# Linear attention's memory laid out anew in a hybrid decoder step: gates, values, queries and keys over r's weights and buffers, W_o's pieces over the prompt attention's last buffers

## The chip, the core and the metric

The kernel runs on one core of one Trainium2 chip. The metric is the device time of the program in microseconds (us), the median of several runs; lower is better. TensorE (PE) does the matrix products, VectorE (DVE), ScalarE (ACT) and GpSimd (POOL) the elementwise work, SyncE (SP) issues most of the DMA transfers.

## What is computed

One layer of a decoder on a prompt of 2048 tokens (width 1024) and 8 sample tokens, all in float32. One projection of the normalised input is split among sliding-window softmax attention (`q_a`, `k_a`, `v_a`), gated linear attention (`q_g`, `k_g`, `v_g`, a swish gate `u_rg`, a low-rank forget gate `u_lr`). Their outputs are joined, go through `w_o` and a residual, and a SwiGLU network follows.

```python
u_qa, u_ka, u_va, u_qg, u_kg, u_vg, u_rg, u_lr = jnp.split(h @ w_in, idx, axis=-1)
...
log_a = jax.nn.log_sigmoid((u_lr @ w_gla_gate2 + b_gla_gate).astype(jnp.float32)) / GLA_TAU
...
def step(S, inp):                       # per chunk of tokens
    qc, kc, vc, ac = inp
    b = jnp.cumsum(ac, axis=2)
    o_inter = jnp.einsum('nhtd,nhdv->nhtv', qc * jnp.exp(b), S)
    diff = b[:, :, :, None, :] - b[:, :, None, :, :]
    decay = jnp.exp(jnp.where(causal[:, :, None], diff, -jnp.inf))
    scores = jnp.einsum('nhtd,nhsd,nhtsd->nhts', qc, kc, decay)
    o = o_inter + jnp.einsum('nhts,nhsv->nhtv', scores, vc)
...
g = rmsnorm(o_gla.astype(x.dtype), gla_norm_g).reshape(N, T, GLA_WIDTH) * jax.nn.silu(r_gla)
h = x + jnp.concatenate([o_attn.astype(x.dtype), g], axis=-1) @ w_o
z = rmsnorm(h, ffn_norm_g)
return h + (jax.nn.silu(z @ w_gate) * (z @ w_up)) @ w_down
```

## The kernel before

**Products.** A float32 operand is split into a rounded high part and the rest (`split`: a cast on ACT, L95, and a subtraction on DVE, L96). A dense product is three products into one bank of PSUM (`mm3`): high by high, high by low, low by high, L107, L108 and L109.

**Stages.** The first is prompt attention, 16 blocks of 128 tokens with the sample tokens: q, k and v of each block, the swish gate `r` (its weights lie in `WR`), scores (L358, L359), the exponential (L370), the division by the sum on POOL (L375, tile `S`), transposes of P (L386, bank `ps_p`) whose split halves go to `pT`, and the products with v (L390, L391, bank `po`). An output is scaled on DVE (`o`, L393) and stored (L394). The low-rank part `lr` of each pair of blocks, and `r`, go out to memory (`lr_d`, `r_d`). The second stage is linear attention, 8 pairs of 128 tokens, that is 256 tokens a pair. `front_b` makes what a pair needs: queries and keys (four output tiles of 24 products into `ps_qk`, copied to `qTb` at L700 and `kTb` at L702), the gates (`ps_g`, L719, from `lr`, a tile of three loads from `lr_d`; ACT's L721, L722 read the bank into `la` and `Bt`; L730 sums along the tokens) and the values (48 products into `ps_v` with `WV`, and for the first pair 16 more for the sample tokens, L747). `gla_b` goes through 7 levels (`E`, L797; a product with q on POOL, L811; four products into `ps_l`, L816; the result into `AT`), then makes the output (`po`, L865 from v and `AT`, L868 from the state) and updates the state. The next pair's front is interleaved by the planner. `split_wo` (L767 to L784) loads a piece of W_o into `wro`, splits it into `wohl` and stores it, a piece every half pair. Then come W_o's stage (its first mixed tile `mt` is cast by ACT's L95), the norm, and the network's three products.

**Memory.** SBUF is cut into pools on a left and a right stack. A pool that is closed gives its bytes back, and the next stage's tiles lie on them. The kernel opens its pools with `reuse_waits="tile"`: a tile over a closed pool's memory waits for the accesses of exactly the old tiles that lay at its bytes. Where a tile is laid therefore sets what it has to wait for.

**Order.** The order of each engine's queue isn't written by hand. A planner simulates the program (`schedule_with_timeline_sim=True`) and puts each engine's instructions into one queue by its own times; an engine then works off its queue in order, and an instruction that waits holds those behind it.

**Lines of the change.** L593 to L609 open the pools of linear attention; L652 to L669 make its constant tiles, among them `AT` (zeroed at L662), the two `lr` tiles `lr30` and `lr31` of 96 by 264 elements (L666, zeroed at L667) and `bd` (L671).

Of the kernel before, what the change touches and what calls it, by code (L numbers as in the profile page):

```python
# [11 lines left out]
F32R = mybir.dt.float32r  # L12
# [39 lines left out]
def hymba_kernel(ctx: ExitStack, tc: tile.TileContext, I, O, X=None, phases=3):  # L52
# [3 lines left out]
    def pool(stack, name, bufs, **kw):  # L56
        return stack.enter_context(tc.tile_pool(name=name, bufs=bufs, reuse_waits="tile", **kw))
# [534 lines left out]
    with ExitStack() as ph:  # L592
        pad = pool(ph, "b_pad", 1)  # L593
# [2 lines left out]
        wl = pool(ph, "b_wl", 2)  # L596
        dp = pool(ph, "b_dec", 1)
        lp = pool(ph, "b_lm", 1)
        gtp = pool(ph, "b_gt", 2)
        wk = pool(ph, "b_wk", 2)  # L600
        qkp = pool(ph, "b_qk", 2)
# [4 lines left out]

        wq1 = pool(ph, "b_wq1", 1, side="right")
        wq0 = pool(ph, "b_wq0", 1, side="right")
        wop = pool(ph, "b_wo", 1)  # L609
        aux = pool(ph, "b_aux", 2, space=PSUM)  # L610
        acc = pool(ph, "b_acc", 2, space=PSUM)
        lvp = pool(ph, "b_lv", 2, space=PSUM)
# [50 lines left out]
            ATs.append(AT)  # L663
        lr3s = []
        for i in range(2):
            lr3 = pad.tile([96, 264], F32R, name=f"lr3{i}")  # L666
            nc.gpsimd.memset(lr3.bitcast(F32), 0.0)  # L667
            lr3s.append(lr3)
        for i in range(3):  # L669
# [777 lines left out]
```

## Time and profile before

| | |
|---|---|
| median of 3 runs | 2285.05 us (2284.72 to 2285.94) |
| the profiled execution | 2284.49 us, its span 2282.5 us |
| PE, DVE, ACT, POOL busy | 97%, 69%, 44%, 27% of the span |
| end of attention's last product to the first gate product | 406.07 to 411.54 |
| first output product of linear attention | 448.75 |
| first product of W_o's stage | 727.14 |

Times inside the execution count from the start of the span, and a program's lines are those of the kernel above. A busy share alone doesn't say whether an engine is held: for that one reads the waits, a list of who waited for whom and how long, and the timeline, which has each instruction's start, its length, and in brackets the idle time just before it with what ended it. Instructions of a kind that follow each other stand in one row with a count.

### The profile page before, as it was taken

How to read it: one execution, taken by the hardware profiler on the slowest of the kernel's cores; microseconds unless marked ns; L12 is line 12 of the kernel's file. 1: busy time of each engine (PE TensorE's matmuls, PEld its weight loads, DVE VectorE, ACT ScalarE, POOL GpSimd, SP SyncE). 2: the span in 40 equal slices, each digit the busy share in tenths (PEclk: the TensorE clock that was granted, in tenths of full speed). 3: DMA queues.
4: the chain of work that ended last, by engine and by line, in shares of the span. 5: the costliest groups of instructions: out<-in, count | busy, mean ns of one | idle time of the engine just before them, and what ended most of it. 6: DMA issues, size and time to landing. Idle time of an engine off the chain costs nothing.

```text
span 2282.5 us, 34902 instructions
## 1 busy us (share of the span) xinstructions
PE 2206.6 (97%) x12697; PEld 1908.8 (84%) x12697; DVE 1567.7 (69%) x3076; ACT 1009.3 (44%) x2259; POOL 625.3 (27%) x706
## 2 busy tenths in 40 slices
PE   8999998899998999999999999999999899999997
PEld 6888887688897788688888889999999878787886
DVE  6787888567766466776666667676676675747486
ACT  5666777465565334332333333333333333434342
POOL 2443433455465133211111111011110122222222
PEclk9999999899999999999999999999999999999999
DMA  7323334245424889944242366233333377878777
GB/s 236 120 77 103 108 104 163 91 132 187 144 88 188 303 291 314 320 137 127 81 124 81 114 222 240 89 107 97 94 103 93 126 200 172 216 171 227 162 203 239
DMA packets 211992, 364.75 MB, mean 160 GB/s; under 512 B 15683, under 2 KB 129116, under 8 KB 208732
## 3 DMA queue, kind: packets, MB, share of 16 engines
q1 hardware_dynamic: 174764, 259.05, 34.7%
q0 software_dynamic: 37056, 103.47, 17.8%
q8 instruction: 100, 1.64, 0.3%
q14 instruction: 72, 0.59, 0.1%
HBM read 211.24 MB, written 152.29 MB: 159 GB/s over the span
## 4 chain that ended last, share of the span: by engine, by line
PE 82%; DMA 5%; DVE 5%; issue 3%; POOL 2%; ACT 2%; SPq 0%; POOLq 0%; DVEq 0%; ACTq 0%
PE ps_b L108 8%; PE ps_b L107 8%; PE ps_b L109 8%; PE ps_c L108 5%; PE ps_c L107 5%; PE ps_c L109 5%; PE ps_a L108 5%; PE ps_a L107 5%; PE ps_a L109 5%; PE ps_d L107 3%; PE ps_d L108 3%; PE ps_d L109 3%; PE ps_wo L107 3%; PE ps_wo L109 3%; PE ps_wo L108 2%
## 5 line engine op out<-in xcount | busy, mean ns | idle before, releaser
L109 PE MATMUL ps_b<-z,whl 128*128 128x258 f32 (+1 forms) x792 | 253.6, 320 | 2.1 <-DVE whl L96 2.1
L107 PE MATMUL ps_b<-z,whl 128*128 128x258 f32 (+1 forms) x792 | 254.3, 321 | 1.2 <-ACT whl L95 1.2
L108 PE MATMUL ps_b<-z,whl 128*128 128x258 f32 (+1 forms) x792 | 254.5, 321 | 0.0
L95 ACT CAST dm<-mr 128x384 fp32r<-128x384 f32 (+1 forms) x224 | 108.1, 488 | 190.6 <-PE ps_b L109 100.6
L108 PE MATMUL ps_a<-z,whl 128*128 128x258 f32 (+1 forms) x528 | 169.4, 321 | 0.0
L108 PE MATMUL ps_c<-z,whl 128*128 128x258 f32 (+1 forms) x528 | 169.4, 321 | 0.0
L109 PE MATMUL ps_a<-z,whl 128*128 128x258 f32 (+1 forms) x528 | 169.2, 320 | 0.0
L109 PE MATMUL ps_c<-z,whl 128*128 128x258 f32 (+1 forms) x528 | 169.1, 320 | 0.0
L107 PE MATMUL ps_c<-z,whl 128*128 128x258 f32 (+1 forms) x528 | 168.9, 320 | 0.2 <-DMA z<-zc_d_P 0.2
L107 PE MATMUL ps_a<-z,whl 128*128 128x258 f32 (+1 forms) x528 | 169.0, 320 | 0.0
L109 PEld LDWEIGHTS ps_b<-z,whl 128*128 128x128 f32 x792 | 149.6, 189 | 14.5 <-DVE whl L96 2.5
L107 PEld LDWEIGHTS ps_b<-z,whl 128*128 128x128 f32 x792 | 149.7, 189 | 13.0 <-ACT whl L95 1.3
L108 PEld LDWEIGHTS ps_b<-z,whl 128*128 128x128 f32 x792 | 149.6, 189 | 11.9
L96 DVE TENSOR_TENSOR dm<-mr,dm 128x384 fp32r<-128x384 f32 (+1 forms) x224 | 115.4, 519 | 61.4 <-ACT dm L95 61.4
L95 ACT CAST whl<-wrg 128x512 fp32r<-128x512 f32 x132 | 81.6, 620 | 155.7 <-PE ps_b L109 81.2
L983 DVE TENSOR_TENSOR gu<-ps_c,gu 128x512 f32<-128x512 f32 (+1 forms) x130 | 77.9, 600 | 56.7 <-PE ps_c L109 56.1
L96 DVE TENSOR_TENSOR whl<-wrg,whl 128x512 fp32r<-128x512 f32 x132 | 90.8, 689 | 36.6 <-ACT whl L95 36.2
L811 POOL TENSOR_TENSOR bd<-E,qTb 64x256 f32<-64x256 f32 x112 | 103.2, 922 | 44.3 <-DVE ebl L840 15.7
L1282 POOL DMA_DIRECT2D md_d<-m x22 | 15.6, 711 | 363.5 <-DVE m L1245 363.5
L95 ACT CAST whl<-sy 128x512 fp32r<-128x512 f32 x88 | 54.6, 620 | 132.2 <-PE ps_b L109 84.9
L107 PEld LDWEIGHTS ps_c<-z,whl 128*128 128x128 f32 x528 | 100.0, 189 | 8.5 <-issue 0.6
L107 PEld LDWEIGHTS ps_a<-z,whl 128*128 128x128 f32 x528 | 100.0, 189 | 7.9
(399 smaller groups left out, 6684.7 us busy)
## 6 DMA issues: line engine op xcount, KB each, us to landing
mr<-md_d SPq DMA_DIRECT2D x24, 1344.0 KB
zc_d_P<-zhl POOLq DMA_DIRECT2D x56, 512.0 KB, 6.4
z<-zc_d_P SPq DMA_DIRECT2D x14, 2048.0 KB
wrg<-in_w_gate_dram SPq DMA_DIRECT2D x44, 512.0 KB
wrg<-in_w_up_dram SPq DMA_DIRECT2D x44, 512.0 KB
nT_d<-nT SPq DMA_DIRECT2D x16, 1024.0 KB
zT<-nT_d SPq DMA_DIRECT2D x8, 2048.0 KB
h_d<-gu POOLq DMA_DIRECT2D x48, 256.0 KB, 4.7
```

Source lines behind the costliest of these rows:

```text
L95: nc.scalar.copy(h, src)
L96: (eng or nc.vector).tensor_tensor(l, src, h.bitcast(F32), ALU.subtract)
L107: nc.tensor.matmul(ps, lh, rh, start=start, stop=False, skip_group_check=more)
L108: nc.tensor.matmul(ps, lh, rl, start=False, stop=False, skip_group_check=more)
L109: nc.tensor.matmul(ps, ll, rh, start=False, stop=stop, skip_group_check=more)
L811: nc.gpsimd.tensor_tensor(bv[rows, h], E5[rows, :, :, 1], qv[rows, :, :, 1], ALU.mult)
L983: nc.vector.tensor_tensor(out, a, b, ALU.add)
L1282: nc.gpsimd.dma_start(md_d[sb][g][:, :, q, fp - GROUPS[g][0], :], src.rearrange("p (m t) -> p m t", m=4))
```

## The change

The pool `wop` of W_o's pieces (`wro`, `wohl`) is opened behind `lp` on the left stack, and no longer behind `wbv`, at the stack's top. Behind it a new pool, `lrp`, holds the two `lr` tiles, which lay in `pad` at the stack's bottom. Every other tile of linear attention on the left stack shifts. The computation is the same, and every instruction has its counterpart. Lines of the changed kernel stand 3 higher from L599 to L608, and 2 higher from L610 on.

```diff
@@ -596,6 +596,9 @@
         wl = pool(ph, "b_wl", 2)
         dp = pool(ph, "b_dec", 1)
         lp = pool(ph, "b_lm", 1)
+        wop = pool(ph, "b_wo", 1)
+
+        lrp = pool(ph, "b_lr", 1)
         gtp = pool(ph, "b_gt", 2)
         wk = pool(ph, "b_wk", 2)
         qkp = pool(ph, "b_qk", 2)
@@ -606,7 +609,6 @@
 
         wq1 = pool(ph, "b_wq1", 1, side="right")
         wq0 = pool(ph, "b_wq0", 1, side="right")
-        wop = pool(ph, "b_wo", 1)
         aux = pool(ph, "b_aux", 2, space=PSUM)
         acc = pool(ph, "b_acc", 2, space=PSUM)
         lvp = pool(ph, "b_lv", 2, space=PSUM)
@@ -663,7 +665,7 @@
             ATs.append(AT)
         lr3s = []
         for i in range(2):
-            lr3 = pad.tile([96, 264], F32R, name=f"lr3{i}")
+            lr3 = lrp.tile([96, 264], F32R, name=f"lr3{i}")
             nc.gpsimd.memset(lr3.bitcast(F32), 0.0)
             lr3s.append(lr3)
```

The bytes in each partition, and the tiles of prompt attention that lay there:

| tile | before | on | after | on |
|---|---|---|---|---|
| `lr30`, `lr31` | 28544 | bias | 91136 | 64 bytes of `rt`, `ks` |
| `scm` | 80960 | `qT` | 93248 | `ks`, `r` |
| `la` | 81984 | `qT`, `o` | 94272 | `r` |
| `Bt` | 84096 | `o`, `ol` | 96384 | `r`, `WR` |
| `v` | 88320 | `ol`, `rt`, `ks`, `r` | 100608 | `WR` |
| `qTb` | 96512 | `r`, `WR` | 108800 | `WR` |
| `kTb` | 100736 | `WR` | 113024 | `WR` |
| `WV` | 104960 | `WR`, `nT` | 117248 | `WR`, `nT` |
| `wro` | 137728 | `nT` | 78848 | `qT` |
| `wohl` | 141824 | `nT`, `qs`, `qn` | 82944 | `qT`, `o`, `ol`, `rt` |

`AT`, `bd`, `r`, `E` and their neighbours move 2112 bytes down. In W_o's stage, whose addresses stay, the first `mt` (113760 to 122016) lay on `WV` alone and now lies on `kTb` and `WV`.

The planner makes another order of this. On PE, around the first gate products (`ps_g`) and the first value products (`ps_v`), before:

```order
L386 MATMUL ps_p<-ident,S 128x128 x4
L391 MATMUL po<-pT,vp_194 128x512
L386 MATMUL ps_p<-ident,S 128x128 x4
L390 MATMUL po<-pT,vp_196 128x512
L391 MATMUL po<-pT,vp_196 128x512
L390 MATMUL po<-pT,vp_194 128x512
L391 MATMUL po<-pT,vp_194 128x512
L719 MATMUL ps_g<-lr_5008,w_130 128x264 x2
L107 MATMUL ps_v<-WV,zT 128x512
L108 MATMUL ps_v<-WV,zT 128x512
L109 MATMUL ps_v<-WV,zT 128x512
```

After:

```order
L386 MATMUL ps_p<-ident,S 128x128 x4
L721 MATMUL ps_g<-lr_5011,w_130 128x264 x2
L358 MATMUL ps_s<-kT_191,qT 128x256
L359 MATMUL ps_s<-kT_191,qT 128x256
L358 MATMUL ps_s<-kT_191,qT 128x256
L359 MATMUL ps_s<-kT_191,qT 128x256
L390 MATMUL po<-pT,vp_195 128x512
L391 MATMUL po<-pT,vp_195 128x512
L390 MATMUL po<-pT,vp_196 128x512
L107 MATMUL ps_v<-WV,zT 128x512
L108 MATMUL ps_v<-WV,zT 128x512
L109 MATMUL ps_v<-WV,zT 128x512
```

The gates and the values stood behind all of attention's products; now the gates stand ahead of its last four score products, and the values ahead of its last products with v.

On POOL, around the zeroing of the two `lr` tiles (`S`, `den` is attention's softmax, `r`, `rt` the swish gate), before:

```order
L375 TENSOR_TENSOR S<-S,den 128x1024 x2
L247 TENSOR_TENSOR r<-r,rt 128x512
L375 TENSOR_TENSOR S<-S,den 128x1024 x4
L658 MEMSET Sbd 128x512
L662 MEMSET AT_5004 128x1024
L662 MEMSET AT_5006 128x1024
L667 MEMSET lr_5008 96x264
L667 MEMSET lr_5010 96x264
```

After:

```order
L375 TENSOR_TENSOR S<-S,den 128x1024 x2
L247 TENSOR_TENSOR r<-r,rt 128x512
L375 TENSOR_TENSOR S<-S,den 128x1024 x2
L669 MEMSET lr_5011 96x264
L669 MEMSET lr_5013 96x264
L375 TENSOR_TENSOR S<-S,den 128x1024 x2
L660 MEMSET Sbd 128x512
L664 MEMSET AT_5007 128x1024
L664 MEMSET AT_5009 128x1024
```

The zeroing of `lr` moved ahead of the last two softmax products; that of `Sbd` and `AT` stays behind them.

On SP, around the loads of `lr` (`mix_d` is where attention's outputs go, `zT` the normalised tokens of a pair, `lm` the level mask), before:

```order
L682 DMA zT<-nT_d_66 128x16x256
L394 DMA mix_d_86<-o 128x512
L394 DMA mix_d_87<-o 128x512
L394 DMA mix_d_88<-o 128x512
L685 DMA lr_5008<-lr_d_89 16x256 x2
L644 DMA lm<-in_c_lmask_dram 128x448
L685 DMA lr_5008<-lr_d_89 16x256
```

After:

```order
L684 DMA zT<-nT_d_66 128x16x256
L687 DMA lr_5011<-lr_d_89 16x256 x2
L394 DMA mix_d_86<-o 128x512
L687 DMA lr_5011<-lr_d_89 16x256
L687 DMA lr_5013<-lr_d_90 16x256 x3
L687 DMA lr_5011<-lr_d_91 16x256 x3
L394 DMA mix_d_87<-o 128x512
L684 DMA zT<-nT_d_67 128x16x256
L766 DMA vdec_d<-v 8x512
L394 DMA mix_d_88<-o 128x512
```

Two loads of the first pair's `lr` are now ahead of the last three stores of attention, those of three pairs ahead of the last two, and the load of the second pair's tokens and the store of the sample tokens' values stand among them. The first load of W_o (L782), which stood before these rows, is now behind them.

On ACT, around the copies of `kTb`, which clear the banks that the gates use (L370 is attention's exponential, `pT` the split of P, `ol` a copy of an output), before:

```order
L700 ACTIVATE qTb<-ps_qk 128x264 x2
L370 ACTIVATE S,den<-S,nm 128x256 x4
L372 ACTIVATE es<-es 128x4
L95 CAST pT<-ps_p 128x512
L702 COPY kTb<-ps_qk 128x264
L392 COPY ol<-po 64x512
L95 CAST pT<-ps_p 128x512
L370 ACTIVATE S,den<-S,nm 128x256 x4
L372 ACTIVATE es<-es 128x4
L702 COPY kTb<-ps_qk 128x264
L95 CAST pT<-ps_p 128x512
L392 COPY ol<-po 64x512
```

After:

```order
L95 CAST lr_5011<-lrTdec 16x8
L704 COPY kTb<-ps_qk 128x264
L370 ACTIVATE S,den<-S,nm 128x256 x4
L372 ACTIVATE es<-es 128x4
L704 COPY kTb<-ps_qk 128x264
L95 CAST pT<-ps_p 128x512
L392 COPY ol<-po 64x512
L95 CAST pT<-ps_p 128x512
L723 ACTIVATE la<-ps_g,nbT 128x256
L724 ACTIVATE Bt<-ps_g,bT 128x256
```

The second `kTb` copy stands behind one block of exponentials in both; the gates' reads of their banks (`la`, `Bt`) moved ahead of attention's last block of exponentials. Of the two `qTb` copies, further ahead, the first moved from behind four casts of `WV` to behind the first of them.

## Rows read from the trace of the kernel before

**Rows 1.** The profile page's first part: busy time, share of the span and instructions of each engine, of the whole execution.

```profile
PE 2206.6 (97%) x12697; PEld 1908.8 (84%) x12697; DVE 1567.7 (69%) x3076; ACT 1009.3 (44%) x2259; POOL 625.3 (27%) x706
```

**Rows 2.** The view by stretches: start and end of the stretch, its length, busy time (and count of instructions) of PE, of PE's weight loads, of DVE, ACT and POOL, the mean clock granted to PE (1.00 is 2.4 GHz), the share of time the DMA engines were busy, and GB/s.

```profile
380.64:430.31 49.67, 37.73 (x185) 30.23 (x184) 29.26 (x74) 25.21 (x67) 16.12 (x18) 0.83 0.32 102
430.31:489.00 58.69, 55.96 (x427) 51.95 (x426) 37.26 (x64) 32.61 (x77) 32.97 (x31) 1.00 0.38 122
400.00:410.00 10.00, 4.71 (x16) 3.37 (x16) 4.89 (x20) 2.54 (x6) 4.69 (x9) 0.67 0.18 60
410.00:420.00 10.00, 7.44 (x23) 5.82 (x24) 4.64 (x9) 5.66 (x15) 0.00 (x0) 0.65 0.52 164
```

**Rows 3.** PE's waits from 380.64 to 430.31: who waited for whom, us in total, times, the longest.

```profile
PE ps_g L719 <- DMA lr<-lr_d: 5.5, 1, 5.5
PE po L390 <- DVE o L393: 3.4, 2, 2.4
PE ps_qk L107 <- ACT qTb L700: 2.0, 1, 2.0
```

**Rows 4.** The view by stretches for PE and one output tile at a time, in this order: `ps_v` (values), `ps_qk` (queries and keys), `po` (attention's products with v), `ps_p` (transposes), `ps_s` (scores). Columns: length, busy time (count), granted clock, DMA share, GB/s.

```profile
380.64:430.31 49.67, 16.77 (x64) 0.83 0.32 102
380.64:430.31 49.67, 8.90 (x51) 0.83 0.32 102
380.64:430.31 49.67, 7.91 (x20) 0.83 0.32 102
380.64:430.31 49.67, 5.43 (x32) 0.83 0.32 102
380.64:430.31 49.67, 1.99 (x12) 0.83 0.32 102
```

**Rows 5.** PE's timeline: start, length, engine, line, operation, tiles, shape and count. The first two rows are 27 products apart with no other work between, the next two 12; the last row is four transposes.

```profile
419.31 0.39 PE L107 MATMUL ps_v<-WV,zT 128*128 128x512 f32 x1
425.56 0.39 PE L107 MATMUL ps_v<-WV,zT 128*128 128x512 f32 x1
373.50 0.28 PE L109 MATMUL ps_qk<-zT,W 128*128 128x264 f32 x1
374.96 0.28 PE L109 MATMUL ps_qk<-zT,WQ 128*128 128x264 f32 x1
396.66 0.60 PE L386 MATMUL ps_p<-ident,S 128*128 128x128 f32 x4
```

**Rows 6.** PE's timeline at the seam of the two stages: the last q product of the second output tile, attention's last product, the first gates, the first value product, and the level products behind the sample tokens' values.

```profile
380.64 0.28 PE L109 MATMUL ps_qk<-zT,WQ 128*128 128x264 f32 x1
405.67 0.40 PE L391 MATMUL po<-pT,vp 128*128 128x512 f32 x1
411.54 0.78 PE L719 MATMUL ps_g<-lr,w 96*128 96x264 f32 x2 [5.47 <-DMA lr<-lr_d]
413.34 0.79 PE L107 MATMUL ps_v<-WV,zT 128*128 128x512 f32 x1 [1.02 <-ACT Bt L722]
430.40 1.50 PE L816 MATMUL ps_l<-bd,E 128*128 128x128 f32 x12
```

**Rows 7.** POOL's timeline: the last product of the swish gate r, two of attention's last softmax products, and the zeroing of `lr`.

```profile
372.33 1.29 POOL L247 TENSOR_TENSOR r<-r,rt 128x512 f32<-128x512 f32 x1 [0.93 <-POOL S L375]
383.25 1.89 POOL L375 TENSOR_TENSOR S<-S,den 128x1024 f32<-128x1024 f32 x1 [7.36 <-DVE den L374]
398.63 1.89 POOL L375 TENSOR_TENSOR S<-S,den 128x1024 f32<-128x1024 f32 x1 [4.53 <-DVE den L374]
402.71 0.58 POOL L667 MEMSET lr<- 96x264 f32 x2
```

**Rows 8.** SP's queue of DMA issues: attention's last three stores (the start is that of the first), and the first pair's last `lr` load.

```profile
388.59 19.16 SPq L394 DMA_DIRECT2D mix_d<-o  x3
409.20 0.42 SPq L685 DMA_DIRECT2D lr<-lr_d  x1
```

**Rows 9.** ACT's timeline: the first exponential of attention's last block but one, the copy of `kTb` behind that block, and the first and the last of the gates' short reads of a bank.

```profile
389.46 0.51 ACT L370 ACTIVATE S<-S,nm 128x256 f32<-128x256 f32 x1 [3.49 <-DVE es L367]
392.08 0.38 ACT L702 COPY kTb<-ps_qk 128x264 f32<-128x264 f32 x1
412.13 0.47 ACT L721 ACTIVATE la<-ps_g,nbT 128x256 f32<-128x256 f32 x1 [5.24 <-PE ps_g L719]
414.02 0.31 ACT L722 ACTIVATE Bt<-ps_g,bT 128x8 f32<-128x8 f32 x1
```

**Rows 10.** DVE's timeline: the subtractions that start the levels of the first and of the second pair.

```profile
417.77 2.50 DVE L797 TENSOR_TENSOR E<-Bt 128x512 f32<-128x512 f32 x4
464.66 2.50 DVE L797 TENSOR_TENSOR E<-Bt 128x512 f32<-128x512 f32 x4
```

**Rows 11.** PE's timeline: the first output products of the first and of the second pair.

```profile
448.75 1.16 PE L865 MATMUL po<-v,AT 128*128 128x128 f32 x8 [1.01 <-DVE AT L826]
488.13 0.61 PE L865 MATMUL po<-v,AT 128*128 128x128 f32 x4
```

**Rows 12.** The end of linear attention: POOL's last product with k, ACT's cast of W_o's first mixed tile, and the view of the tile `wohl` (the casts of W_o's pieces: count, shortest, median and longest in ns, first and last start).

```profile
719.98 1.27 POOL L847 TENSOR_TENSOR kd<-kd,kTb 128x512 f32<-128x512 f32 x1
720.75 1.03 ACT L95 CAST mt<-mr 128x1024 fp32r<-128x1024 f32 x1
L95 ACT CAST wohl<-wro x8: 1030/1036/1045, 477.1 to 631.5; 128x1024 fp32r<-128x1024 f32 x8
```

## The prediction

> **What bounds the kernel now.** I read the page first: TensorE (PE) is busy 97% of the span [rows 1], so a change that moves no work onto or off PE can only pay where PE waits or runs slowly. The change concerns the seam between prompt attention and linear attention, so I looked there, at the stretch from the last q product of the second output tile (380.64) to the first level product behind the sample tokens' values (430.40) [rows 6]. The view by stretches gives PE 37.73 us of work in 49.67 at a mean granted clock of 0.83, and in 400 to 420 a clock of 0.67 and 0.65: part of the time at 1.2 GHz instead of 2.4, around the longest waits [rows 2]. PE's waits there are three: the gates for the load of `lr` (5.5 us), attention's products for `o` (3.4), the q/k products for the copy of `qTb` (2.0) [rows 3].
>
> How much of the 49.67 is work? I take the counts by tile [rows 4], each at the start-to-start distance that its form has at full clock [rows 5]. 64 products into `ps_v` and 20 into `po` have 512 columns: 27 steps from 419.31 to 425.56, 0.2315 each, 19.4 together. 51 into `ps_qk`: 12 steps from 373.50 to 374.96, 0.122 each, 6.2. 32 transposes into `ps_p`: four in 0.60, of which about 0.27 is the last one's own length, 0.11 each, 3.5. 12 into `ps_s`, taken as `ps_qk`, 1.5; gates and four level products 0.7. The sum is 31.3. **The stretch loses 18.4 us.** Behind it, from 430.31 to 489, PE's busy column leaves only 2.7 of 58.7 open at clock 1.00 [rows 2]: linear attention runs at PE's pace.
>
> The busy column by itself would give a smaller loss, 49.67 - 37.73 = 11.9, and the weight-load column a larger one, 49.67 - 30.23 = 19.4 [rows 2]. The Trainium skill (Perfetto Trace Analysis, Identifying the Most-Contended Engine) says that matmul busy time is a poor measure because products are pipelined, and weight-load time the better one. By the first column the gain below would be 6.5 us smaller, by the second 1.0 larger; the count by distances agrees with the skill.
>
> **The change part by part.** No arithmetic is added or removed. What moves is what a tile of linear attention has to wait for, and with it the planner's order.
>
> *Gates and values, earlier.* Before, `lr30` and `lr31` lie on attention's bias, `la`, `Bt` and part of the values on its outputs `o` and `ol`. So the zeroing of `lr` stands on POOL at 402.71, behind the last softmax product at 398.63 [rows 7]; its last load goes out at 409.20, behind three stores of `o` [rows 8]; the gates start at 411.54 and the values at 413.34, when attention's last product (405.67) is long done [rows 6]. Afterwards these tiles lie on r's weights and buffers, whose last product on POOL is at 372.33 [rows 7]. The order shows what follows: the zeroing goes ahead of the last two softmax products, two `lr` loads ahead of all three stores, the gates ahead of attention's last four score products, and the 48 + 16 value products among attention's last ones. That is the work PE lacked.
>
> *When do the gates start?* Ahead of them PE now has 48 q/k products, 8 of `po`, 16 transposes and 8 scores: 10.5 us by rows 5, so it arrives at 391. The second of POOL's last four softmax products ended at 385.14 [rows 7]; with 0.6 for the zeroing and 2.3 for a load (issued 409.20, used 411.54) two thirds of `lr` are there by 388. The last third is behind the first store, which went out at 388.59 [rows 8]: 391 too. No wait of note. The q/k wait for `qTb` (2.0) goes as well, since that copy moves ahead of three casts of `WV` in ScalarE's order.
>
> *What stays lost.* The second gate product needs a bank that the copy of `kTb` frees, and on ScalarE that copy is behind four exponentials of attention. These and a cast took from 389.46 to 392.08, the copy 0.38 [rows 9]; with their maxima ready at 391 the bank is free at about 393.4, so PE waits 2 us. Then attention's products need the previous `o` and the split of P, and the values a gate's bank, which ScalarE clears in the 2.2 us from 412.13 to the end of the row at 414.02 [rows 9]: some 2 us more, beside each other. I take 4 us. Bounds: nothing, where ScalarE's queue runs ahead; 12.8, where attention's four last output groups each cost 1.7 (3.4 for two [rows 3]), the bank 2, and the clock falls to 1.2 GHz for 8 of the 13 or so us that 0.67 and 0.65 stand for, at half a microsecond each. I take the low side because the waits that remain are short ones with work between. The skill (TensorE: Matmul & The Clock Gate, What's actually happening) has the clock low by default and raised by activity; rows 2 agree, with 1.00 behind 430.31 where PE is fed.
>
> *The levels.* The subtraction that starts them (`E`, 417.77 [rows 10]) waits, before and after, for attention's last `o`, since VectorE is in order. That `o` moves back with the values ahead of it on PE: 391, 4 of waiting, some 21 of products, 416. So `E` starts about where it did. This costs nothing while PE has other work, and it has: the new order puts the next pair's q/k products (96 x 0.122 = 11.7) ahead of the first level and the next pair's values (48 x 0.2315 = 11.1) among the levels. The first pair's output products start little earlier than 448.75 [rows 11], but with the values done besides. From the second pair's (488.13 [rows 11]) to the W_o stage both orders hold the same work ahead of each pair's output, within 1.5 us by rows 5, so the lead stays. The second pair's levels began at 464.66 [rows 10]; `E` for them now stands ahead of the first pair's output on VectorE, so they can follow.
>
> *SP.* The `lr` loads of three pairs now stand ahead of the last two stores of `o`; the third pair's waits for the first pair's gates (391 to 394), before those stores are ready, so nobody behind (lmask, r, states) is held. The first W_o load moves behind the last store, to about 418; its first cast was at 477.1 [rows 12]. Nothing.
>
> *W_o's seam.* The first mixed tile `mt` now lies on `kTb`, so its cast (720.75) must wait for POOL's last product with k, 719.98 to 721.25 [rows 12]. 0.5 us; bounds 0 and 1.3. W_o's loads still wait for the last values, and move with them. AT and bd shift by 2112 bytes, and are zeroed behind the last softmax product as before: nothing.
>
> **Sum.** 18.4 - 4.0 - 0.5 = 13.9, so 14 us, carried to the end because the later stages follow in the same order. The profiled execution took 2284.49, 0.56 under the median of 2285.05: 2270.5 there, 2271.0 as a median.
>
> **Rivals.** *The chain binds, not PE.* If VectorE, ScalarE and POOL set the pace of the first pair, only the start of `E` counts, which moves by 0 to 3 us: 2282 to 2285. For it: from `E` to the first output 31 us pass, 417.77 to 448.75. Against: PE is open for 2.7 us of 58.7 there [rows 2]. 0.10.
>
> *Most of the wait comes back.* The gates stand ahead of attention's last products in PE's one queue. If each wait of attention's tail is paid again, as in the upper bound, 12.8 of the 18.4 stay: a gain of 5, 2280. 0.14.
>
> *Slower.* If `lr` comes as late as before, at 411.54, everything behind the gates waits: 21 us of products and 4 of waits end at 436.5, not 430.4, and the kernel takes 2292. It decides at 405: an `lr` load used later than that loses. The path is SP's queue, with the last third of `lr` behind a store of attention. Against: that store went out at 388.59 [rows 8], and nothing that it needs is delayed by more than a microsecond or two. 0.05.
>
> *All is won.* No wait stays, and the 2.7 us behind the stretch go too: 18.4 + 2.7 - 0.5, 2264. 0.11.
>
> *It doesn't do what it says*: the gates would still stand behind attention. In the order they don't, so it has no chance of its own.
>
> **How the numbers follow.** The forecast, a gain of 9 to 18 us, has 0.60. A measurement of this kernel can tell about 0.2% from no change, 4.6 us, so faster means under 2280.5. Faster: 0.60 + 0.11 + 0.10 of *most comes back* = 0.81. Same: 0.10 + the other 0.04 = 0.14. Slower: 0.05. The range of 2263 to 2280 takes in *all is won*, the forecast and the better part of *most comes back*, 0.80.
>
> **What would show it.** Right: gates near 391 and values from about 397; granted clock above 0.9 in 380 to 420; PE's wait for `lr` under 1 us; the sample tokens' values done near 416; the second pair's output products near 474; the first W_o product near 713 instead of 727. Wrong: if the W_o stage starts near 727 although the values came early (the chain binds), or if PE waits more than 8 us in all between 385 and 416.

## The result and the profile after

| | before | after |
|---|---|---|
| median | 2285.49 us (2284.72 to 2286.32, 4 runs) | 2265.26 us (2264.08 to 2266.95, 4 runs) |
| profiled execution, its span | 2284.49, 2282.5 us | 2265.43, 2263.7 us |
| first product of W_o's stage | 727.14 | 709.69 |

The ratio is 0.9917 (0.9905 to 0.9929): 20.2 us faster by the medians, 19.1 by the two profiled executions. The forecast was 2271.0 in a range of 2263 to 2280.

The view by stretches of the changed kernel, with the columns of [rows 2], shows the seam:

```profile
380.64:430.31 49.67, 47.12 (x297) 40.58 (x296) 28.98 (x75) 28.55 (x78) 17.74 (x20) 0.97 0.49 148
400.00:410.00 10.00, 10.00 (x51) 8.19 (x50) 4.87 (x6) 2.29 (x5) 4.71 (x7) 1.00 0.07 26
410.00:420.00 10.00, 10.00 (x66) 7.83 (x65) 5.67 (x16) 4.40 (x10) 0.00 (x0) 1.00 0.74 235
430.31:489.00 58.69, 54.12 (x364) 47.29 (x363) 44.93 (x77) 33.44 (x84) 32.20 (x32) 0.97 0.30 92
```

In the first stretch PE does 297 products instead of 185, and the granted clock in 400 to 420 is 1.00 instead of 0.67 and 0.65. The last row shows the other side: behind the seam PE is now open for 4.6 us at a mean granted clock of 0.97, where it had 2.7 open at 1.00.

PE's waits in that first stretch, with the columns of [rows 3]:

```profile
PE ps_g L721 <- ACT kTb L704: 1.6, 1, 1.6
PE po L390 <- DVE o L393: 0.9, 1, 0.9
```

The 5.5 us for the load of `lr` and the 2.0 for `qTb` are gone. PE's timeline at the gates and the values, as in [rows 6]; the last row is the sample tokens' 16 products:

```profile
390.81 0.37 PE L721 MATMUL ps_g<-lr,w 96*128 96x264 f32 x1
392.78 0.39 PE L721 MATMUL ps_g<-lr,w 96*128 96x264 f32 x1 [1.60 <-ACT kTb L704]
...
394.59 0.50 PE L390 MATMUL po<-pT,vp 128*128 128x512 f32 x1 [0.94 <-DVE o L393]
...
395.54 0.62 PE L107 MATMUL ps_v<-WV,zT 128*128 128x512 f32 x1
395.96 0.63 PE L108 MATMUL ps_v<-WV,zT 128*128 128x512 f32 x1
...
411.22 3.85 PE L749 MATMUL ps_v<-WV,nTdec 128*40 128x512 f32 x16
```

The gates start 20.7 us earlier. The zeroing of `lr` on GpSimd, of [rows 7], now begins at 386.54 us, and SP issues the first two loads at 386.88:

```profile
386.54 0.58 POOL L669 MEMSET lr<- 96x264 f32 x2 [1.39 <-issue]
```

```profile
386.88 0.81 SPq L687 DMA_DIRECT2D lr<-lr_d  x2
387.74 0.41 SPq L394 DMA_DIRECT2D mix_d<-o  x1
388.20 6.23 SPq L687 DMA_DIRECT2D lr<-lr_d  x7
```

**Where the time came from.** I summed PE's products from 355 us on, each at the distance of its form ([rows 5]; level products at 0.105, as the 12 of [rows 6] from 430.40 to 431.66), and compared when each kernel had done the same amount:

| work done, us | before was there at | after earlier by | what lies there |
|---|---|---|---|
| 20 | 389.2 | 4.5 | q/k products, no wait for `qTb` |
| 40 | 423.9 | 14.0 | the seam |
| 60 | 445.5 | 15.7 | first pair's levels in the kernel before |
| 90 | 477.0 | 10.8 | second pair's levels |
| 130 | 518.9 | 8.1 | third pair's levels |
| 160 | 555.8 | 13.8 | fourth pair's levels |
| 250 | 653.6 | 14.1 | |
| 300 | 706.9 | 15.7 | last pair |
| 320 | 739.8 | 17.4 | W_o's stage |

The seam gives 14.0, and the first pair's levels 1.7 more. Then 7.6 of the lead is lost up to the third pair's levels, 5.7 comes back up to the fourth's, and 3.6 more by W_o's stage, most of it in the last pairs. A trace is one execution: where two kernels below have the same order, their rows differ by up to 2.6 us, so that a single row tells less than the table's large steps.

The loss: the same 70 us of work, from the first pair's levels to the third's, take 73.4 us in the kernel before and 81.0 in the changed one (the view by stretches, in this order):

```profile
445.50:518.90 73.40, 71.75 (x514) 64.42 (x513) 49.67 (x90) 46.92 (x117) 41.10 (x41) 1.00 0.41 133
429.80:510.80 81.00, 75.78 (x527) 66.96 (x526) 64.47 (x108) 50.23 (x123) 50.82 (x49) 0.98 0.39 129
```

PE is open for 1.6 us of the first and 5.2 of the second. The changed kernel's timeline shows waits of 0.84, 0.68 and 1.21 us for VectorE's writes of `AT`, 1.48 and 0.65 for `bd`, and its clock falls:

```profile
452.49 0.49 PE L818 MATMUL ps_l<-bd,E 128*128 128x128 f32 x2 [1.48 <-POOL bd L813]
470.40 1.13 PE L818 MATMUL ps_l<-bd,E 128*128 128x128 f32 x8 [1.21 <-DVE AT L828]
```

```profile
440.00:460.00 20.00, 17.36 (x121) 15.75 (x122) 17.22 (x29) 10.16 (x25) 10.47 (x12) 0.91 0.34 106
```

A mean of 0.91 over 20 us is 3.6 us at 1.2 GHz, 1.8 us of PE's work. With the 3.6 us more of open time that is 5.4 of the 7.6; the rest isn't traced.

The gain up to the fourth pair's levels: the kernel before waits 2.18 us for `bd` there and then runs at 0.66, which the changed kernel, whose longest wait between 500 and 690 is 0.8, does not.

```profile
549.94 1.90 PE L816 MATMUL ps_l<-bd,E 128*128 128x128 f32 x8 [2.18 <-POOL bd L811]
```

```profile
550.00:555.00 5.00, 5.00 (x31) 5.00 (x32) 1.56 (x3) 1.84 (x3) 4.62 (x6) 0.66 1.07 391
```

In the kernel before, GpSimd's first `bd` of this pair stands in its queue behind `eB` (q times its decay, for the product with the state) and `rs_r`, the root of a normalisation of the pair ahead:

```profile
545.55 1.47 POOL L841 TENSOR_TENSOR eB<-eB,qTb 128x512 f32<-128x512 f32 x1 [3.38 <-DVE rs_v L114]
546.99 1.19 POOL L115 TENSOR_TENSOR rs_r<-rs_v,nhalf 128x4 f32<-128x4 f32 x1
548.15 7.12 POOL L811 TENSOR_TENSOR bd<-E,qTb 64x256 f32<-64x256 f32 x8
```

In the changed kernel the root is done ahead of `eB`, and `bd` starts at 535.56:

```profile
534.30 1.30 POOL L843 TENSOR_TENSOR eB<-eB,qTb 128x512 f32<-128x512 f32 x1 [2.61 <-DVE ebl L842]
535.56 12.52 POOL L813 TENSOR_TENSOR bd<-E,qTb 64x256 f32<-64x256 f32 x12
```

VectorE's waits from 415 to 735 changed as well. Before, it stood 28.1 us for the gates of the pairs; after, 7.2, and more for PE's output products. That this is why PE waits less is likely; no run separates it.

```profile
DVE la L726 <- ACT Bt L725: 28.1, 7, 5.4
DVE ob L886 <- PE po L868: 17.8, 9, 2.7
```

```profile
DVE ob L888 <- PE po L870: 26.8, 10, 5.8
...
DVE la L728 <- ACT Bt L727: 7.2, 5, 3.8
```

### The profile page after: what moved, and what is told of

Same layout as the page of the kernel before. It is cut to its first block, busy times and chain, and to the rows that moved or that the text cites. A ratio compares the mean times of both kernels' runs of the same rounds, so it can differ in the third digit from the quotient of the medians.

```text
span 2263.7 us, 34888 instructions
## 1 busy us (share of the span) xinstructions
PE 2201.3 (97%) x12697; PEld 1903.6 (84%) x12697; DVE 1566.6 (69%) x3076; ACT 1006.7 (44%) x2259; POOL 624.7 (28%) x706
## 4 chain that ended last, share of the span: by engine, by line
PE 69%; issue 17%; POOL 6%; DVE 4%; DMA 2%; ACT 1%; SPq 0%; POOLq 0%; DVEq 0%; ACTq 0%
PE ps_b L108 6%; PE ps_b L107 6%; PE ps_b L109 6%; PE ps_c L108 4%; PE ps_c L107 4%; PE ps_c L109 4%; POOL h_d L1380 4%; PE ps_a L108 4%; PE ps_a L107 4%; PE ps_a L109 4%; PE ps_d L107 3%; PE ps_d L109 3%; PE ps_d L108 3%; PE ps_wo L107 2%; PE ps_wo L109 2%
## 5 line engine op out<-in xcount | busy, mean ns | idle before, releaser
L109 PE MATMUL ps_b<-z,whl 128*128 128x258 f32 (+1 forms) x792 | 253.4, 320 | 2.1 <-DVE whl L96 2.1
L109 PE MATMUL ps_a<-z,whl 128*128 128x258 f32 (+1 forms) x528 | 168.9, 320 | 0.0
L109 PE MATMUL ps_c<-z,whl 128*128 128x258 f32 (+1 forms) x528 | 168.9, 320 | 0.0
L109 PEld LDWEIGHTS ps_b<-z,whl 128*128 128x128 f32 x792 | 149.5, 189 | 14.6 <-DVE whl L96 2.5
L1284 POOL DMA_DIRECT2D md_d<-m x22 | 15.7, 713 | 363.5 <-DVE m L1247 363.5
```

Of the source, the lines that this page charges most:

```text
L109: nc.tensor.matmul(ps, ll, rh, start=False, stop=stop, skip_group_check=more)
L1284: nc.gpsimd.dma_start(md_d[sb][g][:, :, q, fp - GROUPS[g][0], :], src.rearrange("p (m t) -> p m t", m=4))
```

## The experiments

**Half of the change: `lr` back on the bias.**

```diff
-            lr3 = lrp.tile([96, 264], F32R, name=f"lr3{i}")
+            lr3 = pad.tile([96, 264], F32R, name=f"lr3{i}")
```

> The change with the two lr tiles back in the pool at the stack's bottom, over attention's bias; gates, values, queries and keys stay over r's weights and buffers, W_o's pieces over attention's last buffers. Theory (the earliest start of the gates is set by whichever of lr and la comes last, so one half of the change alone gives nothing): the zeroing of lr stands behind the last softmax product again, the gates start at 410 to 412, the stretch 400 to 420 has a granted clock below 0.75, and the time is 2283 to 2288. Rival (the two halves add up, the values' place being worth the larger part because 64 value products could run without the gates): 2270 to 2278.

2286.80 us, ratio to the kernel before 1.0013 (1.0003 to 1.0023). PE's first gates in it:

```profile
411.40 0.78 PE L720 MATMUL ps_g<-lr,w 96*128 96x264 f32 x2 [5.78 <-DVE lmask L646]
```

**The other half: W_o's pieces back at the top, `lr` in its new pool.** `wop` is opened behind `wq0` again; `lr` then lies on attention's `qT`, and `la`, `Bt` and the values on `o` and `ol`.

> The change with W_o's pieces back at the stack's top, so that la, Bt and the values lie on attention's outputs o and ol again, and lr on attention's qT. Theory (both must be early): la and Bt wait for the stores of attention's outputs, the gates and values stand behind all of attention's products, and the time is 2281 to 2287. Rival (the halves add up): 2270 to 2278.

2283.79 us, ratio 0.9993 (0.9983 to 1.0002). PE's first gates in it:

```profile
412.65 0.78 PE L721 MATMUL ps_g<-lr,w 96*128 96x264 f32 x2 [6.66 <-DMA lr<-lr_d]
```

Both are within 0.2% of the kernel before, at a granted clock of 0.62 and 0.59 over 400 to 420. The halves don't add up, and the whole 20 us needs both. In the first run `lr` is late: GpSimd zeroes it at 402.62, and its last load goes out at 408.75. (The row puts the wait down to VectorE's cast of the level mask, `lmask`, which ended at 411.39.) But `lr` is late in the second run too, zeroed at 404.04 and loaded from 408.74 on, behind all of attention's stores. So a late `lr` is shown to be enough; that the old place of `la` and `Bt` by itself would hold the gates is not.

**The seam with W_o's stage.**

```diff
-            qT = qkp.tile([P, 2, 264], F32, tag="qT", name="qTb")
             kTt = qkp.tile([P, 2, 264], F32, tag="kT", name="kTb")
+            qT = qkp.tile([P, 2, 264], F32, tag="qT", name="qTb")
```

> The change with kTb laid out ahead of qTb, so that W_o's first mixed tile lies on qTb and the values' weights, and not on kTb. In the changed kernel its cast waited 2.7 us on ScalarE for GpSimd's last product with k, at 704.3. Theory (the cast's wait lies beside PE's last levels and costs nothing): 2264 to 2267, the first W_o product within 1 us of 709.7. Rival (the cast is on the path, as the prediction's seam term of 0.5 us has it): 2262 to 2264, first W_o product 1 to 2.7 us earlier.

2265.29 us, ratio 0.9917 (0.9902 to 0.9932), the same as the changed kernel. ScalarE's cast of the first `mt`, in the changed kernel and then in this one:

```profile
705.62 1.04 ACT L95 CAST mt<-mr 128x1024 fp32r<-128x1024 f32 x1 [2.72 <-POOL kd L849]
```

```profile
703.70 1.05 ACT L95 CAST mt<-mr 128x1024 fp32r<-128x1024 f32 x1 [1.38 <-POOL bd L813]
```

The cast comes 1.9 us earlier and the first W_o product 0.7 (708.96), as the second pair's first output product already did (477.71 against 478.42), and the kernel's time stays. The wait for `kTb` lay beside PE's last levels.

**Less work for PE in the first pair.** Of the sample tokens' 16 value products two are left.

```diff
-                        for k in range(KD):
+                        for k in range(1):
                             for hl in range(2):
                                 nc.tensor.matmul(ps[:40], nTdec[:, k], WV[:, hl, k], ...)
```

> The change with 2 instead of 16 products for the sample tokens' values (14 products left out, so the sample tokens' values are those of one slice of the input alone). At the distance of 0.2315 us of such products that is 3.2 us of PE's work in the first pair. Theory (PE sets the pace from the seam to W_o's stage): 2261 to 2263. Rival (the levels' chain through VectorE, ScalarE and GpSimd sets the pace of the first two pairs, so that work taken from PE there only makes it wait longer): 2264.5 to 2266.

2267.40 us, ratio 0.9926 (0.9911 to 0.9941), against 0.9917 for the changed kernel: no gain, and above both ranges. The first pair's output products come at 448.73 instead of 453.11, the second pair's are already where they were:

```profile
478.25 0.61 PE L867 MATMUL po<-v,AT 128*128 128x128 f32 x4
```

```profile
478.42 0.71 PE L867 MATMUL po<-v,AT 128*128 128x128 f32 x4
```

So 3.2 us less of PE's work did not shorten the kernel, and the forecast of 2261 to 2263 fell. What became of them isn't shown: the planner made another order of this kernel, on PE from 412 us on. The third pair's output products come 6.7 us earlier than in the changed kernel (509.56 against 516.22), and the first W_o product 0.7 later (710.40). That the order took back what the work gave is a rival to *the chain covers PE's work*.

**Less work for VectorE among the levels.** Two of the three passes that make each sample token's state are left out, in the changed kernel and in the kernel before.

```diff
-                nc.vector.tensor_tensor(vb, vb, dec_k[:, :, n:n + 1].to_broadcast([P, 2, P]), ALU.mult)
-                nc.vector.tensor_tensor(S0, S0, vb, ALU.add)
```

> The changed kernel without two of the three VectorE steps of each sample token's state (the product of its key and value and its addition are left out, so the sample tokens' states and outputs are wrong in value). Five of these 16 steps, about 4 us, stand among the first pair's levels on VectorE at 429.8 to 439.5. PE's order up to the first pair's outputs stays as it is. Theory (in the first pairs of the changed kernel the chain of the levels through VectorE, ScalarE and GpSimd sets the pace, since PE has run ahead): 2260 to 2263, PE's first output product at 448 to 451 instead of 453.1. Rival (PE sets the pace all the way, and the run with two sample products was slower by the planner's other order): 2264 to 2266, first output product within 1 us of 453.1.

> The kernel before without the same VectorE steps (left out as in the run beside it). Theory (in the kernel before PE, late with its values, sets the pace of the first pairs, so that VectorE's work there is covered): 2284 to 2286, the first output product at 448 to 449 as it was. Rival (the chain through VectorE paces the first pairs there too): 2280 to 2283.

The changed kernel without them takes 2257.48 us, ratio 0.9887 (0.9872 to 0.9902), 7.8 less than with them by the medians and 6.9 by the ratios, more than forecast. PE, VectorE, ScalarE and GpSimd work in the order of the changed kernel but for a few rows, so this is what the passes cost there: their time on VectorE, and the 3.7 us in which VectorE's queue stands for the load of `vb` ahead of them. The first output products come at 449.83, but that alone says little, as the run with the last pair's product below shows.

The kernel before takes 2267.81, ratio 0.9928 (0.9914 to 0.9943): 16.6 us less than the 2284.45 measured beside it, where I had expected nothing and the rival 2 to 5. At equal work its lead over the kernel before is -0.8 at the seam (gates at 410.23), 2.2 at the third pair's levels, 7.2 at the fourth's, 12.5 at the end. The passes hold VectorE in that kernel for 8.2 us and make it wait 5.8 for a load (whole lines by group from 360 to 735; behind the bar the busy time, the mean of one in ns, the idle time before them):

```profile
L928 DVE TENSOR_TENSOR vb<-vb,dec_k 128x256 f32<-128x256 f32 x8 | 4.1, 513 | 5.8 <-DMA vb<-vdec_d 5.7
L929 DVE TENSOR_TENSOR S<-S,vb 128x256 f32<-128x256 f32 x8 | 4.1, 507 | 0.0
```

Here the order did change. Up to about 530 us all four engines work in that of the kernel before but for a few rows, and up to there the lead is 2.2. From the fourth pair on it is another: GpSimd makes that pair's first two `bd` ahead of `eB`, and PE's wait of 2.18 us is gone.

```profile
538.56 1.56 POOL L811 TENSOR_TENSOR bd<-E,qTb 64x256 f32<-64x256 f32 x2 [1.82 <-DVE E L797]
540.32 1.31 POOL L841 TENSOR_TENSOR eB<-eB,qTb 128x512 f32<-128x512 f32 x1 [0.20 <-DVE ebl L840]
```

So the chain of the levels through VectorE holds PE in the changed kernel. In the kernel before the passes cost some 3 us up to the third pair's levels, little more than executions differ by; how much of the rest of the 16.6 is the passes and how much the planner's new order isn't shown.

**Both taken away** from the changed kernel: the edits of the fourth and the fifth experiment together.

> The changed kernel with 2 instead of 16 products for the sample tokens' values and without the two VectorE steps of each sample token's state. Theory (the chain sets the pace of the first pairs, and behind it PE; each work taken away alone is partly covered by the other): 2257 to 2261, less than the run without the VectorE steps alone. Rival (PE's work there is covered whatever VectorE does): the time of the run without the VectorE steps alone, within 1 us.

2254.28 us, ratio 0.9872 (0.9856 to 0.9889): 3.2 us less than without the passes alone, which is what the 14 products take at their distance (14 x 0.2315). It is below the theory's range, and the rival (no gain) fell. With VectorE's passes in place the same 14 products had given nothing. That would make it a matter of a few us of VectorE's work which of PE and the chain paces the first pairs. It is not shown, since the order on PE differs from 412 us on from that of the run without the passes alone, as it did in the run with two sample products; the agreement with 3.2 may be chance.

**The end of linear attention.** In the last pair the product of q and k goes to VectorE.

```diff
-            nc.gpsimd.tensor_tensor(qk, qT[:, :, 0:256], k2, ALU.mult)
+            (nc.vector if pp == NB // 2 - 1 else nc.gpsimd).tensor_tensor(qk, qT[:, :, 0:256], k2, ALU.mult)
```

> The changed kernel with the last pair's product of q and k on VectorE instead of GpSimd, where it stands for 1.7 us ahead of the root that the last normalisation but one waits for; PE waits 5.2 us for that at 693.8 to 698.9, the longest wait between the seam and W_o's stage. Theory (this wait is on the path): 2262.5 to 2264, wait 3 to 4 us. Rival (VectorE, or the six products with q behind it on GpSimd, take it up): 2264.5 to 2266.

2262.03 us, ratio 0.9904 (0.9889 to 0.9919). PE's wait for the last normalisation but one, in the changed kernel and in this one:

```profile
698.94 0.48 PE L902 MATMUL ps_m<-ident,r 128*128 128x128 f32 x1 [5.17 <-ACT r L898]
```

```profile
695.72 0.48 PE L902 MATMUL ps_m<-ident,r 128*128 128x128 f32 x1 [4.47 <-ACT r L898]
```

It ends 3.2 us earlier, 0.7 of it the wait itself (3 to 4 us of wait were forecast, 4.47 are left), and the first W_o product comes at 706.33, 3.4 earlier. But most of that was there long before the edit. Up to 690 us the four engines work in the changed kernel's order, and yet the first pair's output products come 2.6 us earlier:

```profile
453.11 1.48 PE L867 MATMUL po<-v,AT 128*128 128x128 f32 x8
```

```profile
450.53 1.16 PE L867 MATMUL po<-v,AT 128*128 128x128 f32 x8
```

The second pair's are 2.6 earlier too (475.86 against 478.42). So 0.8 of the 3.4 us lies where the edit is, and the rest is a difference between two executions. With ratios whose intervals overlap, it isn't shown that this wait is on the path.

**The sample tokens' steps done otherwise**, with the output whole: in the changed kernel, in the one of the last experiment, and in the kernel before.

```diff
-                nc.vector.tensor_tensor(S0, S0, a[:, :, n:n + 1].to_broadcast([P, 2, P]), ALU.mult)
-                nc.vector.tensor_tensor(vb, vb, dec_k[:, :, n:n + 1].to_broadcast([P, 2, P]), ALU.mult)
-                nc.vector.tensor_tensor(S0, S0, vb, ALU.add)
+                for h in range(2):
+                    nc.scalar.activation(vb[:, h], vb[:, h], AF.Copy, scale=dec_k[:, h, n:n + 1])
+                    nc.vector.scalar_tensor_tensor(S0[:, h], S0[:, h], a[:, h, n:n + 1], vb[:, h], ALU.mult, ALU.add)
```

> The changed kernel, whole, with each sample token's state made in other steps: ScalarE multiplies the value by the key (two scaled copies of 128 by 128), VectorE multiplies the state and adds in one pass (two of 128 by 128), instead of three VectorE passes over 128 by 256. Leaving two of the three passes out had given 2257.5. Theory (VectorE's passes among the levels cost time; on ScalarE they lie beside it): 2257 to 2261. Rival (ScalarE is in the same chain, Abs and Exp of each level, and holds it as long): 2263 to 2267.

> The same, and the last pair's product of q and k on VectorE, which alone gave 2262.0. Theory (the two waits are at different ends of linear attention and add up): 2254 to 2258. Rival (the end of linear attention is reached in another order, so the second gain is lost): as the run beside it, within 1 us.

> The kernel before with the sample tokens' steps of these two runs. Leaving two of the passes out had given 2267.8 there, 16.6 us less. Theory (these passes cost more in the kernel before, where each pair's values come late and the chain has no lead to spend): 2268 to 2276, and the change is then worth 10 to 14 us instead of 20. Rival (the sample steps and the seam are separate costs): the change is worth 18 to 21 us with the new steps too, so 2277 to 2282.

2264.31, 2260.73 and 2275.11 us; ratios 0.9909 (0.9896 to 0.9923), 0.9894 (0.9880 to 0.9909), 0.9957 (0.9944 to 0.9969). In the changed kernel the new steps give 1 us, as the rival had it: the wait for the load of `vb` is now ScalarE's, 4.4 us. The move at the end takes the median 3.6 further down, short of the 2254 to 2258 of theory; the intervals overlap, and at the first W_o product the two traces are 1.1 us apart (708.46 and 707.37). In the kernel before the new steps give 10.5 us, so that with them the change is worth 2275.11 - 2264.31 = 10.8, as theory had it. Half of what the change brings is therefore time that the kernel before could also have won at another place. Here too the planner put `bd` ahead of `eB` in the fourth pair (541.64 and 543.86), so steps and order aren't separated.

**E's buffers on the bias.** One more move of memory: a pool of E's four buffers at the stack's bottom, AT in its turn behind `bd`.

```diff
-        pc = pool(ph, "b_const", 1)
+        ep = pool(ph, "b_e", 4)
         bdp = pool(ph, "b_bd", 1)
+        pc = pool(ph, "b_const", 1)
...
-                E = wl.tile([P, 2, 256], F32, tag="E", name="E", bufs=4)
+                E = ep.tile([P, 2, 256], F32, tag="E", name="E")
```

> The changed kernel with one more move of memory: the four buffers of E, which lay on attention's S, go to the stack's bottom on attention's bias and first keys, and AT takes their turn behind bd, on the last keys, values and S. In the planner's order three of the first pair's four first subtractions now stand ahead of attention's last output on VectorE, and the first pair's output products 31 instructions earlier on PE. In the changed kernel E started at 418.05, 16 us behind the sums that it reads, and PE gave back some 6 us of its lead in the first two pairs. Theory (the late start of E is the larger part of that): E at 415 to 417, first output products at 447 to 450 instead of 453.1, time 2259 to 2262.5. Rival (the chain's own length sets the pace of the first pairs wherever it starts within a few us): 2264 to 2267.

2273.05 us, ratio 0.9932 (0.9919 to 0.9946): 7.8 above the changed kernel's median, 3.4 by the ratios, whose intervals overlap, and outside what either theory gave. That it is slower is likely and not shown. Its trace is of the slowest of its six runs, 2281.53 us, so it shows more loss than the median has. E starts at 417.28, 0.8 earlier, and the first output products at 447.14, 6.0 earlier; but the third pair's come 6.5 later, behind a wait that the changed kernel doesn't have, with a clock of 0.83:

```profile
522.77 1.22 PE L868 MATMUL po<-v,AT 128*128 128x128 f32 x4 [2.53 <-DVE AT L829]
```

```profile
520.00:540.00 20.00, 17.47 (x84) 13.50 (x83) 11.35 (x25) 9.97 (x28) 3.20 (x4) 0.83 0.32 107
```

At equal work its lead over the kernel before is 8.7 behind the second pair, like the changed kernel's 8.1, and falls to 2.2 in the third. An early first output is no gain by itself: in this order a later wait takes it back. Whether a truly earlier E would save the loss of the first two pairs stays open, since E moved by only 0.8 us, less than two executions of one order differ (E at 415.47 in the run with the last pair's product on VectorE).

## Why the prediction held, and where it was off

- **The start of the gates and values.** Right: 391 forecast, 390.81 measured; the second gate product waits 1.6 us for the copy of `kTb` (2 forecast), attention's products 0.9 for `o`; values at 395.54 (397 forecast); the sample tokens' values end at 415.07 (416 forecast). Neither half of the change alone brings it.
- **What stays lost, 4.0 of 18.4.** Right in sum, by luck in part: the forecast was two waits of 2 us each. The waits are 2.5 us, and to them come nine value products at 0.42 instead of 0.2315 us behind them (395.54, 395.96), 1.7 us, the clock at half, which the forecast put only into its upper bound. The bound of 12.8 was far off, since no wait of attention's tail was longer than 1.6 us.
- **The seam, 13.9.** 14.0 at equal work, so the count by distances was the right measure of PE's work. The Trainium skill (Perfetto Trace Analysis, Identifying the Most-Contended Engine) puts weight-load time, beside the share of peak work, in the place of matmul busy time. The run agrees with its measured 14.0: by the busy column the forecast gain would have been 7.4 (11.9 less the 4.0 and 0.5 that were to stay), by the weight-load column 14.9 (19.4 less the same).
- **The levels, carried to the end without loss or gain.** This step failed. It rested on the open 2.7 us of PE behind the seam, from which I took PE to set the pace. Where PE had run ahead it came to wait for `AT` and `bd`: 7.6 us of the lead went between the first and the third pair's levels, and the second pair's output products came at 478.42, not near 474. The run without VectorE's passes, in the same order, shows that VectorE's chain takes part of it: its lead at the third pair's levels is 11.6 instead of 8.1, where the other two traces in this order have 7 to 9; some 0.8 of it was there at the seam. The rival *the chain binds* had this mechanism with a wrong price, since it supposed that only the start of `E` counts. The step also took the kernel before to lose nothing behind the seam. That kernel loses time there, 3.9 us at the fourth pair's `bd` alone (a wait of 2.18 and 1.7 of clock), and the changed kernel is spared it: its lead grows by 5.7 us up to that point, and by 3.6 more by W_o's stage. Both the run without the passes (16.6 us) and the one with the new steps (10.5) win time in the kernel before from the same pair on, in another order of GpSimd. That it is the same time as the change's is argued from its place; no run separates it. The loss of 7.6 and the gains of 1.7, 5.7 and 3.6 partly cancel, which is luck: the profiled execution gained 19.1 us, 5 more than forecast.
- **W_o's seam, -0.5.** No cost found: without that wait, in the run with `mt` on the queries, the time is the same.
- **Behind W_o.** 17.45 us at its first product, 18.8 at the span's end. The remaining 1.35 lies in W_o's stage itself: from its first product to the start of its last L109 product it lasts 199.5 us before (to 926.6) and 198.1 after (to 907.8). The traces of the other runs have 195.7 to 201.0 there, so this is no more than executions differ by.
- **Rivals.** *Slower* wanted `lr` late in an order that has it early; `lr` came in time. *Most comes back* fell at the seam, where 4 and not 12.8 stayed. *All is won* (2264) is nearest the measured time, for another reason than it gave.

Of the kernels with whole output the fastest is the one with both moves, 2260.73 us: 0.9894 of the kernel before against 0.9917. The intervals overlap, so that it beats the changed kernel is likely and not shown.

## What to carry to other kernels

Where tiles wait for the memory under them, ask of every tile that starts a stage what lay there and when that was last touched; moving one of two such tiles gives nothing while the other still waits. A gain at a seam has to be followed through the stages behind it at equal work: a lead on one engine can be spent on waits for another engine's chain, and a PE that looks full doesn't say that it sets the pace. To learn which engine does, take a known piece of work from each alone and from both, and compare the order of every engine's queue before you read the difference: where a planner orders the program anew, an edit changes the order too. Look as well for what an edit can't have touched: a row ahead of it that moved as far as the row behind it says that the two executions differ, not the kernels.

## What had not been expected of the hardware

Where PE waits for such a chain it pays a second time in its clock: after the wait of 2.18 us at 549.94 the granted clock is 0.66 over the next 5 us, 1.7 us of work at 1.2 instead of 2.4 GHz. Taking 16 VectorE passes out of the kernel before saved 16.6 us, more than the 8.2 us that they are busy and the 5.8 that VectorE waits ahead of them together; the planner's new order has a share in it that isn't known. And two executions in the same order on the four engines differed by 2.6 us at the first pair's outputs (453.11 and 450.53).
